# The FoX stage of a hybrid decoder block: engine order fixed by the source, weights as a stream of pieces, softmax in steps, heads as a pipeline, five gate units plain

## The chip, the cores and the metric

The kernel runs on one core of one Trainium2 chip. The time is the device time of one execution in microseconds (us), on that core. A core has five engines with a queue of their own each: TensorE (PE; matmuls, with PEld for its weight loads), VectorE (DVE), ScalarE (ACT), GpSimd (POOL) and SyncE (SP, which here only issues DMAs). In this kernel's programs every engine takes its instructions in the order of its own queue, and an instruction at the head that waits holds up all that stand behind it on that engine.

## The reference

One layer of a decoder trunk over 512 tokens behind 16 meta tokens, model width 1024. A normalised input `h` goes through one wide projection, whose columns are the inputs of two branches and of their gates:

```python
h = rms_norm(x, g_pre)
z = h @ w_in
(fq, fk, fv, ff, fz, mqk, mv, mi, mf, mo, mz, ga, gb) = jnp.split(z, SPLIT_POINTS, axis=-1)
oa = forgetting_attention(fq, fk, fv, log_fa)
ya = (oa * jax.nn.silu(fz)) @ w_a
hb = rms_norm(jax.nn.sigmoid(mo) * mlstm_scan(...), g_head)
yb = (hb * jax.nn.silu(mz)) @ w_b
merged = jax.nn.sigmoid(ga) * ya + jax.nn.sigmoid(gb) * yb
return x + rms_norm(merged @ w_o, g_post)
```

`forgetting_attention` (FoX) is causal softmax attention of 8 heads of 128, with a decay `cum[t] - cum[s]` added to the scores. The mLSTM branch has 4 heads with a matrix memory in chunks of 128.

## The kernel before

Everything is held transposed, channels on the 128 partitions and tokens along the free axis. Each fp32 operand is split into two parts of a shorter format, a high one (`_h`, a copy by ScalarE) and a low one (`_l`, a subtraction by VectorE), and a product is three matmuls, high by high, high by low and low by high (`mm3`, L148). A weight tile thus goes by DMA into a raw buffer (names in `_r`), through ScalarE and VectorE (`wsplit`, L141 and L143), and then to TensorE.

A block of 256 output columns over 512 tokens can be made in two ways. **Plain**: two banks of 512 columns, 2 x 8 x 3 = 48 matmuls of 512 columns. **Seven products** (`st_narrow`, L254, and `st_products`, L288): Strassen's scheme, 7 products of 12 matmuls of 256 columns, in the order X, Y, Z, W, Y, X, Z, on two banks. The weights are then split in four blocks, a to d; between them stand sums of raw blocks, two on GpSimd (L259, L260, before block b) and two on VectorE (L265, L266, before block d). Between the products ScalarE copies half-finished banks into a snapshot: a wide one behind the second product (512 columns, L313), a narrow one behind W (256 columns, L317) and one behind the second X (L321). A later product writes into the copied bank and has to wait for the copy. At the end VectorE combines the banks with the snapshots (L324, L325, L327).

The program runs the mLSTM branch head by head, with the blocks of `mz` (`mz_part`, L766) as seven-product units in it, then turns the last head's result (`turn_part`, L809) and comes to the FoX stage (L1018 on). This makes, with units of seven products for `fq`, `fz`, `ga` and `gb`, four pairs of heads: `fq_part` and `fk_part` (queries and keys of two heads), `fv_part` (values of four), then for each head the steps of the softmax:

- `prob_part` (L940): scores on TensorE (names `pl`); for each of four blocks of queries VectorE adds the decay `ab` and takes the least value (L959; the signs are turned), ScalarE takes the exponential (L964, with a running sum), VectorE the reciprocal (L965), and the product with it is written by GpSimd (a small part, L967) and VectorE (the rest, L969) into `pn`;
- `ptr_part` (L972): TensorE transposes `pn` into four banks `pt` and one `pmt`, ScalarE makes the high part `pth` (L986) and VectorE the low one `ptl` (L987);
- `fout_part` (L992): the product with the values (`pfo`), multiplied into `yb` by VectorE (L1005).

The gates' results wait in DRAM (`d_yb`, `d_sa`). After the stage come the product with `w_a` (names `pya`) and the output projection. Eight PSUM banks turn round among all of these; a bank is free when its last reader is done.

What sets the order: the source gives a program, and the framework's scheduler sorts the instructions of each engine by its own priorities, in front of the run. The order of the lines is a wish; buffers bind it (four raw buffers, four of `whi`, four of `wlo`, one of `whs` for block a).

## Time and profile before

| | us |
|---|---|
| median of 3 runs | 959.43 |
| lowest and highest | 958.69, 959.86 |
| the profiled execution's own time | 958.12 |
| its span | 956.3 |
| mLSTM part of the span, 110 to 516.8: length, PE busy | 406.80, 401.40 |
| tail, 861.1 to the end: length, PE busy | 95.20, 88.52 |

The profiled execution took 958.12 us, 1.8 us more than the span of its records. Times within the trace count from the span's start. The FoX stage begins with the first matmul of `fq0` at 516.8 and ends with the first one of `pya` at 861.1; its row, with the page's totals, is shown where it is used. Engines that overlap each have their own busy time, so these do not add up to the length of a stretch. In a view of waits a row gives who waited, for which instruction, the time in all, how often, and the longest.

### The profile page before, as it was taken

What the parts mean: (1) busy time and instruction counts of PE and PEld (TensorE: products, weight loads), DVE (VectorE), ACT (ScalarE), POOL (GpSimd) and SP (SyncE); (2) the same over time, 40 slices, a digit from 0 to 9 for tenths busy, and PEclk for the clock granted to TensorE, in tenths of its full rate; (3) what the DMA queues carried; (4) which work ended last, traced back from release to release, by engine and by line L of the source; (5) the groups of instructions that cost most, each with busy time, mean ns of one, the idle gap of its engine ahead of it and who ended that gap; (6) DMA issues with size and microseconds to landing.
All of it is one profiled execution on the core that took longest, in us unless ns stands there. A gap on an engine that the chain in (4) does not pass through costs nothing.

```text
span 956.3 us, 15752 instructions
## 1 busy us (share of the span) xinstructions
PE 915.8 (96%) x6296; PEld 844.5 (88%) x6296; DVE 649.0 (68%) x1080; ACT 473.9 (50%) x818; POOL 194.1 (20%) x222
## 2 busy tenths in 40 slices
PE   8999799999999999999999999989899999899997
PEld 6998799889998899988999988889798899798887
DVE  6988598447686276872768665677774676885633
ACT  5746456435565254662545424455653554773331
POOL 3055100120101211012112114223531233410000
PEclk9999999999999999999999999999999999999999
DMA  7323143203223222322223325224342233248402
GB/s 226 91 82 95 45 129 104 88 23 111 88 90 105 61 81 75 113 77 87 73 61 110 112 88 162 62 79 133 102 155 74 73 90 110 89 167 311 145 23 89
DMA packets 73539, 97.47 MB, mean 102 GB/s; under 512 B 5237, under 2 KB 56533, under 8 KB 73466
## 3 DMA queue, kind: packets, MB, share of 16 engines
q1 hardware_dynamic: 71400, 92.76, 31.7%
q0 software_dynamic: 576, 2.10, 0.6%
q10 hardware_dynamic: 1490, 1.61, 0.5%
q8 instruction: 49, 0.80, 0.3%
q14 instruction: 24, 0.20, 0.1%
HBM read 90.62 MB, written 5.83 MB: 101 GB/s over the span
## 4 chain that ended last, share of the span: by engine, by line
PE 73%; DVE 11%; issue 5%; POOL 5%; ACT 4%; DMA 1%; POOLq 0%; DVEq 0%; ACTq 0%
PE pyb L150 3%; PE pyb L151 3%; PE pyb L149 3%; PE pv L151 3%; PE pv L150 3%; PE pv L149 3%; PE po L149 3%; PE po L151 3%; PE po L150 3%; PE pqk L149 3%; PE pqk L151 3%; PE pqk L150 3%; PE pfk L149 2%; PE pfk L151 2%; PE pfk L150 2%
## 5 line engine op out<-in xcount | busy, mean ns | idle before, releaser
L967 POOL TENSOR_SCALAR pn<-lt,rsum 128x128 f32<-128x128 f32 x32 | 31.1, 972 | 108.6 <-DVE rsum L965 58.6
L150 PE MATMUL pyb<-bl,wb_h 128*128 128x512 f32 x128 | 49.9, 390 | 0.0
L151 PE MATMUL pyb<-bh,wb_l 128*128 128x512 f32 x128 | 49.8, 389 | 0.0
L149 PE MATMUL pyb<-bh,wb_h 128*128 128x512 f32 x128 | 49.8, 389 | 0.0
L150 PE MATMUL pv<-wv_l,hh 128*128 128x512 f32 (+1 forms) x128 | 46.6, 364 | 1.5 <-DVE wv_l L143 1.5
L151 PE MATMUL pv<-wv_h,hl 128*128 128x512 f32 (+1 forms) x128 | 46.4, 363 | 0.0
L149 PE MATMUL pv<-wv_h,hh 128*128 128x512 f32 (+1 forms) x128 | 46.4, 363 | 0.0
L694 DVE SCALAR_TENSOR_TENSOR y<-z,gc,y 128x512 f32<-128x512 f32 (+1 forms) x48 | 36.2, 759 | 2.0 <-ACT y L687 1.3
L149 PE MATMUL pqk<-hh,wq_h 128*128 128x258 f32 x128 | 36.4, 284 | 0.0
L149 PE MATMUL pfk<-hh,wfk_h 128*128 128x264 f32 x128 | 36.4, 284 | 0.0
L149 PE MATMUL pqk<-hh,wk_h 128*128 128x264 f32 x128 | 36.3, 284 | 0.0
L151 PE MATMUL pqk<-hh,wk_l 128*128 128x264 f32 x128 | 36.3, 284 | 0.0
L150 PE MATMUL pfk<-hl,wfk_h 128*128 128x264 f32 x128 | 36.3, 284 | 0.0
L151 PE MATMUL pfk<-hh,wfk_l 128*128 128x264 f32 x128 | 36.3, 283 | 0.0
L150 PE MATMUL pqk<-hl,wk_h 128*128 128x264 f32 x128 | 36.3, 283 | 0.0
L150 PE MATMUL pqk<-hl,wq_h 128*128 128x258 f32 x128 | 36.0, 282 | 0.0
L151 PE MATMUL pqk<-hh,wq_l 128*128 128x258 f32 x128 | 36.0, 282 | 0.0
L150 PEld LDWEIGHTS pv<-wv_l,hh 128*128 128x128 f32 x128 | 24.1, 189 | 5.6 <-DVE wv_l L143 1.7
L151 PEld LDWEIGHTS pyb<-bh,wb_l 128*128 128x128 f32 x128 | 24.0, 188 | 5.0
L149 PEld LDWEIGHTS pyb<-bh,wb_h 128*128 128x128 f32 x128 | 24.0, 188 | 4.9
L150 PEld LDWEIGHTS pyb<-bl,wb_h 128*128 128x128 f32 x128 | 24.0, 188 | 4.9
L149 PEld LDWEIGHTS pv<-wv_h,hh 128*128 128x128 f32 x128 | 24.2, 189 | 3.9
(1806 smaller groups left out, 3662.1 us busy)
## 6 DMA issues: line engine op xcount, KB each, us to landing
wv_r<-in_w_in_dram SPq DMA_DIRECT2D x16, 512.0 KB, 4.5
wo_r<-in_w_in_dram SPq DMA_DIRECT2D x16, 512.0 KB, 4.1
wz_r<-in_w_in_dram SPq DMA_DIRECT2D x16, 512.0 KB, 3.7
wb_r<-in_w_b_dram SPq DMA_DIRECT2D x16, 512.0 KB, 3.4
ab<-d_na SPq DMA_DIRECT2D x8, 672.0 KB, 3.8
wq_r<-in_w_in_dram SPq DMA_DIRECT2D x8, 512.0 KB, 3.6
wk_r<-in_w_in_dram SPq DMA_DIRECT2D x8, 512.0 KB, 3.7
wfq_r<-in_w_in_dram SPq DMA_DIRECT2D x8, 512.0 KB, 3.6
```

The costliest lines, as they stand in the source:

```text
L149: T.matmul(ps, ah, bh, start=start, stop=False, **kw)
L150: T.matmul(ps, ah, bl, start=False, stop=False, **kw)
L151: T.matmul(ps, al, bh, start=False, stop=stop, **kw)
L694: V.scalar_tensor_tensor(y[:, t0:L], z[:, m, t0 + j:L + j], gc[:, j * 16 + mi:j * 16 + mi + 1], y[:, t0:L], ALU.mult, ALU.add)
L967: G.tensor_scalar(pn[:, o:o + P].rearrange("p (g t) -> p g t", g=4), lt[:, 0:32].unsqueeze(1).to_broadcast([P, 4, 32]), rsum, None, ALU.mult)
```

## The change

Within the FoX stage, from `fq0` to the last product with `w_a`, each engine now keeps the order in which the source issues its instructions: `V`, `S`, `G` and `T` are wrapped, and each instruction that goes through them is pinned while `order["on"]` is set (in the trace they then all have the wrapper's line, L66).

The weights of the stage and of what follows it are one list of jobs. `loads()` starts the next DMA as soon as a raw buffer is spare, and `pieces()` issues the next piece of the list, a split with what belongs to it, if its buffers are free. `side(n)` stands between products: it takes up to n steps off the queue of the softmax and issues one piece. A unit of seven products calls it seven times, a plain one after each half of a row of products (four k each).

A head's softmax is cut into ten steps. Its scores, and the least value and exponential of the first two query blocks, are issued at once; the other steps go into the queue and are taken between the products that follow. The heads form a pipeline: in step s stand `fout_part` of head s-2, the scores of head s, the transposes of head s-1, and then the units of `INTERVALS[s]` (names with a star are units of seven products). `gb1`, `gb2`, `gb3`, `ga1` and `ga2` have no star: they are plain. The large part of the product with the reciprocal goes from VectorE to ScalarE, and the pair of banks of a unit is read from the second bank first. Snapshots of `fq` go into the buffer `sg` and not into `w`. Ahead of the stage one thing changes: every second block of `mz` puts its split a into `sg`, and four pieces of `fq0` are issued before `turn_part`. Of `w_a` the first block takes k 0 to 5 of both halves before k 6 and 7; the rest of the tail differs only in where its weights are loaded and split.

```diff
-    V, S, G, T = nc.vector, nc.scalar, nc.gpsimd, nc.tensor
+    order = {"on": False}
+
+    class Engine:
+
+        def __init__(self, engine):
+            self.engine = engine
+
+        def __getattr__(self, name):
+            issue = getattr(self.engine, name)
+            return lambda *a, **kw: tc.keep_in_program_order(issue(*a, **kw)) if order["on"] else issue(*a, **kw)
+
+    V, S, G, T = (Engine(e) for e in (nc.vector, nc.scalar, nc.gpsimd, nc.tensor))
...
     def mz_part(h, u):
         g = sb([P, 2, SEQ], F32, ("qk1h", "qk1l")[u], f"gz{h}{u}")
-        ps = st_unit(C_MZ + h * MV + u * 256, f"z{h}{u}", g)
+        ps = banks(f"pz{h}{u}", 2)
+        snap = g.rearrange("p a (b n) -> p (a b) n", b=2)
+        into = None
+        if u:
+            t = sb([P, 2, 4, P], F32R, "sg", f"wz{h}{u}a", gp)
+            into = t[:, 0], t[:, 1]
+        st_products(st_narrow(C_MZ + h * MV + u * 256, f"wz{h}{u}", into), [(ps[0], ps[1], snap, None)])
...
+    class Job:
+        def __init__(self, name, src, k0, nk, c0, nc_, seven=False):
+            self.name, self.src, self.k0, self.nc, self.c0, self.seven = name, src, k0, nc_, c0, seven
+            self.hk = 1024 // nc_
+            self.n = nk // self.hk
+            self.raws, self.done, self.parts = [], 0, {}
+            self.pieces = 4 if seven else self.n
...
+        def piece(self):
+
+            i = self.done
+            pool = "whs" if self.seven and i == 0 else "whi"
+            if not spare[pool] or len(self.raws) < (2 if self.seven else i + 1):
+                return False
+            spare[pool] -= 1
+            if not self.seven:
+                self.parts[i] = split(self.raws[i], f"{self.name}{i}")
+                spare["raw"] += 1
...
+                if i == 0:
+                    self.parts["a11"] = split(r0[:, :, a], f"{self.name}a", ("whs", "wls"), mw, 1)
+                    G.tensor_tensor(r0[:, :, a], r0[:, :, a], r0[:, :, b], ALU.add)
+                    G.tensor_tensor(r0[:, :, b], r0[:, :, b], r1[:, :, b], ALU.add)
+                elif i == 1:
+                    self.parts["s3"], self.parts["s1"] = both(r0, "b")
+                elif i == 2:
+                    self.parts["a12"], self.parts["a22"] = both(r1, "c")
+                    V.tensor_tensor(r1[:, :, b], r0[:, :, a], r1[:, :, b], ALU.add)
+                    V.tensor_tensor(r1[:, :, a], r1[:, :, a], r1[:, :, b], ALU.add)
+                    spare["raw"] += 1
+                else:
+                    self.parts["s4"], self.parts["s2"] = both(r1, "d")
+                    spare["raw"] += 1
+            self.done += 1
+            return True
...
+    INTERVALS = (("gb1",), ("fq1*", "fk1", "fv0", "fz0*"), ("gb2",), ("fq2*", "fk2", "fz1*"), ("gb3",),
+                 ("fq3*", "fk3", "fv2", "fz2*", "fz3*"), ("ga1",), ("ga2",), ("ga3*",))
+    add("gb0*", *(n for i in INTERVALS for n in i))
...
+    def loads():
+        while loading[0] < len(jobs) and spare["raw"]:
+            j = jobs[loading[0]]
+            if len(j.raws) < j.n:
+                j.load()
+                spare["raw"] -= 1
+            else:
+                loading[0] += 1
+
+    def pieces():
+        loads()
+        while splitting[0] < len(jobs) and jobs[splitting[0]].done == jobs[splitting[0]].pieces:
+            splitting[0] += 1
+        ok = splitting[0] < len(jobs) and jobs[splitting[0]].piece()
+        loads()
+        return ok
+
+
+    queue = []
+
+    def side(n=1):
+        if order["on"]:
+            for _ in range(n):
+                if queue:
+                    queue.pop(0)()
+            pieces()
...
+    def plain(job, ps):
+
+        w = job.w()
+        for m in range(2):
+            for k in range(KC):
+                mm3(ps[m], w[0](k, m * P, m * P + P), w[1](k, m * P, m * P + P),
+                    hh[:, k, NM:L], hl[:, k, NM:L], k == 0, k == KC - 1)
+                if k % 4 == 3:
+                    side(3)
+        free(n=2)
+        return ps
...
+        prod("X", "a11", "b11", 0)
+        free("whs")
+        side(2)
+        prod("Y", "s3", "t3", 1)
+        S.activation(snap[:, 0:2], halves(yx), AF.Copy)
+        side(2)
+        prod("Z", "s1", "t1", 1)
+        free()
+        side(2)
+        prod("W", "a12", "b21", 2)
+        S.activation(snap[:, 3], wz[:, 256:512], AF.Copy)
+        side(2)
+        prod("Y", "a22", "t4", 2)
+        free()
+        side()
+        prod("X", "s2", "t2", 3)
+        S.activation(snap[:, 2], yx[:, 256:512], AF.Copy)
+        side()
+        prod("Z", "s4", "b22", 3)
+        free()
+        V.tensor_tensor(yx[:, 256:512], snap[:, 0], yx[:, 256:512], ALU.subtract)
+        V.tensor_tensor(halves(yx), halves(yx), snap[:, 2:4], ALU.subtract)
+        V.tensor_tensor(halves(wz), halves(wz), snap[:, 1:3], ALU.add)
+        side()
+        return ps
...
     def fq_part(p):
-        ps = st_unit(C_FQ + p * 256, f"fq{p}", sb([P, 2, SEQ], F32, "w", f"fqs{p}"))
+        ps = unit(by_name[f"fq{p}"], room(f"fqs{p}"))
...
+        def normal(c):
+            kn, o = ends(c)[-1][1], OFFP[c]
+            S.activation(pn[:, o + P:o + P + kn - NM], lts[c][:, NM:kn], AF.Identity, scale=rsums[c])
...
-            V.tensor_scalar(pn[:, o + P:o + P + kn - NM], lt[:, NM:kn], rsum, None, ALU.mult)
+                            lts[c][:, 0:32].unsqueeze(1).to_broadcast([P, 4, 32]), rsums[c], None, ALU.mult)
...
+        for c in (0, 1):
+            scores(c)
+            least(c)
+            power(c)
+        for c in (2, 3):
+            scores(c)
+        more += [lambda: inverse(0), lambda: normal(0), lambda: (least(2), inverse(1)),
+                 lambda: (power(2), normal(1)), lambda: (least(3), after()), lambda: (power(3), inverse(2)),
+                 lambda: normal(2), lambda: inverse(3), lambda: normal(3)]
+        if h + 1 < FH:
+            more.append(lambda: ab_mask(abs_[h + 1]))
...
+    for _ in range(4):
+        pieces()
+    bt = turn_part(*pend)
+    order["on"] = True
     q = fq_part(0)
+    abs_[0] = ab_load(0)
...
+    ab_mask(abs_[0])
...
     gb_part(0)
...
+    pns, pts, vs = {}, {}, {}
+    gs = []
+    for s in range(FH + 2):
+        flush()
+        if s >= 2:
+            fout_part(s - 2, pts[s - 2], vs[(s - 2) // 4])
+        if s < FH:
+            pns[s] = prob_part(s, q, k, queue)
+        if 1 <= s <= FH:
+            pts[s - 1] = ptr_part(s - 1, pns[s - 1])
+        if s == FH:
+            for p in range(2):
+                gs.append(gsplit(p, (sb([P, 2, SEQ], F32R, f"qk{p}h", f"gh{p}"),
+                                     sb([P, 2, SEQ], F32R, f"qk{p}l", f"gl{p}"))))
+            gs.append(gsplit(2, pair("w", "g2")))
+        for n in INTERVALS[s] if s < len(INTERVALS) else ():
+            kind, u = n[0:2], int(n[2])
+            if kind == "fq":
...
-    sa3 = gate_part(C_GA, 3, "ga")
...
-        w2 = wchunk(wa, 0, KC, u * 256, 256, f"wa{u}")
+        w2 = by_name[f"wa{u}"].w()
...
+        for ks in (range(6), range(6, 8)) if u == 0 else (range(8),):
+            for m in range(2):
...
+    order["on"] = False
```

Three places show how the order moves. In the rows, `wfq1d_h` is the high part of block d of unit `fq1`'s weights, `fqs1` its snapshot, `lt1c`, `mn1c` and `rsum1c` the scores, least value and sum of query block c of head 1, and a number behind the last underscore names the buffer.

**First place: unit `fq1`, ScalarE.** Before:

```order
L927 ACTIVATE sgb1_6586<-pgb1_1_6588 128x512
L249 ACTIVATE wfz1a_h_7033<-wfz10_r0_7029 128x512
L313 ACTIVATE fqs1_6722<-pfq1_1_6724 128x512
L141 ACTIVATE wfk1_h1_6853<-wfk1_r1_6847 128x1024
L317 ACTIVATE fqs1_6722<-pfq1_0_6723 128x256
L249 ACTIVATE wfz1b_h_7039<-wfz10_r0_7029 128x1024
L321 ACTIVATE fqs1_6722<-pfq1_1_6724 128x256
L249 ACTIVATE wfz1c_h_7043<-wfz11_r0_7031 128x1024
```

After:

```order
L66 ACTIVATE pn1_6268<-lt10_6273,rsum10_6276 128x128
L66 ACTIVATE wfq1d_h_6349<-wfq1_r1_6039 128x1024
L66 ACTIVATE fqs1_6331<-pfq1_1_6333 128x512
L66 ACTIVATE lt12_6368,rsum12_6372<-lt12_6368,mn12_6369 128x400
L66 ACTIVATE pn1_6268<-lt11_6282,rsum11_6285 128x256
L66 ACTIVATE wfk10_h_6376<-wfk1_r0_6058 128x1024
L66 ACTIVATE lt13_6394,rsum13_6400<-lt13_6394,mn13_6395 128x528
L66 ACTIVATE wfk11_h_6403<-wfk1_r1_6076 128x1024
L66 ACTIVATE fqs1_6331<-pfq1_0_6332 128x256
```

Before, the narrow snapshot (`fqs1`, 256 columns, from bank 0) had one split between it and the wide one. Now two exponentials (`lt12`, `lt13`), a product with the reciprocal and two splits stand between them.

VectorE at the same place, before:

```order
L251 TENSOR_TENSOR wfq1d_l_6747<-wfq11_r0_6727,wfq1d_h_6745 128x1024
L143 TENSOR_TENSOR wfk1_l0_6851<-wfk1_r0_6845,wfk1_h0_6849 128x1024
L1005 TENSOR_TENSOR yb_75<-pfo1_6707,yb_75 128x512
L251 TENSOR_TENSOR wfz1a_l_7035<-wfz10_r0_7029,wfz1a_h_7033 128x512
L143 TENSOR_TENSOR wfk1_l1_6855<-wfk1_r1_6847,wfk1_h1_6853 128x1024
L251 TENSOR_TENSOR wfz1b_l_7041<-wfz10_r0_7029,wfz1b_h_7039 128x1024
L324 TENSOR_TENSOR pfq1_1_6724<-fqs1_6722,pfq1_1_6724 128x256
```

And after:

```order
L66 RECIPROCAL rsum10_6276<-rsum10_6276 128x1
L66 TENSOR_TENSOR wfq1d_l_6351<-wfq1_r1_6039,wfq1d_h_6349 128x1024
L66 ISA lt12_6368,mn12_6369<-pl120_6287,ab1_6226 128x400
L66 ISA mn12_6369 128x1
L66 RECIPROCAL rsum11_6285<-rsum11_6285 128x1
L66 TENSOR_TENSOR wfk10_l_6378<-wfk1_r0_6058,wfk10_h_6376 128x1024
L66 ISA lt13_6394,mn13_6395<-pl130_6291,ab1_6226 128x264
L66 ISA mn13_6395 128x1
L66 ISA lt13_6394,mn13_6395<-pl131_6295,ab1_6226,mn13_6395 128x264
```

Before, no step of a softmax stood among the low parts of this unit. Now the third and fourth query blocks' least values (the rows `lt12` and `lt13`) stand there, the fourth behind the low part of `wfk10`.

**Second place: the end of unit `fz0` and the step behind it, VectorE.** `pfz0_0` and `pfz0_1` are the unit's banks, `yb_75` takes its result. Before:

```order
L265 TENSOR_TENSOR wgb11_r0_6591<-wgb10_r0_6589,wgb11_r0_6591 128x4x128
L266 TENSOR_TENSOR wgb11_r0_6591<-wgb11_r0_6591 128x4x128
L324 TENSOR_TENSOR pfz0_1_6420<-yb_75,pfz0_1_6420 128x256
L325 TENSOR_TENSOR pfz0_1_6420<-pfz0_1_6420,yb_75 128x512
L327 TENSOR_TENSOR pfz0_0_6419<-pfz0_0_6419,yb_75 128x512
L251 TENSOR_TENSOR wgb1d_l_6611<-wgb11_r0_6591,wgb1d_h_6609 128x1024
L921 TENSOR_TENSOR yb_75<-pfz0_0_6419,yb_75 128x512
L921 TENSOR_TENSOR yb_75<-pfz0_1_6420,yb_75 128x512
L1005 TENSOR_TENSOR yb_75<-pfo0_6539,yb_75 128x512
L987 TENSOR_TENSOR ptl1_6555<-pt10_6558,pth1_6554 128x128
```

After:

```order
L66 TENSOR_TENSOR wfq2a_l_6831<-wfq2_r0_6697,wfq2a_h_6829 128x512
L66 TENSOR_TENSOR wfq2b_l_6849<-wfq2_r0_6697,wfq2b_h_6847 128x1024
L66 TENSOR_TENSOR pfz0_1_6766<-yb_75,pfz0_1_6766 128x256
L66 TENSOR_TENSOR pfz0_1_6766<-pfz0_1_6766,yb_75 128x512
L66 TENSOR_TENSOR pfz0_0_6765<-pfz0_0_6765,yb_75 128x512
L66 TENSOR_TENSOR wfq2c_l_6881<-wfq2_r1_6731,wfq2c_h_6879 128x1024
L66 TENSOR_TENSOR wfq2_r1_6731<-wfq2_r0_6697,wfq2_r1_6731 128x4x128
L66 TENSOR_TENSOR wfq2_r1_6731<-wfq2_r1_6731 128x4x128
L66 TENSOR_TENSOR yb_75<-pfz0_1_6766,yb_75 128x512
L66 TENSOR_TENSOR yb_75<-pfz0_0_6765,yb_75 128x512
L66 TENSOR_TENSOR yb_75<-pfo0_6891,yb_75 128x512
L66 ISA lt20_6911,mn20_6912<-pl200_6907,ab2_6398 128x144
```

The combinations of the banks now stand behind two low parts of the next `fq`, and one low part and two sums stand between them and the products that free the banks. The product of `pfo` and the least value of head 2 come next, ahead of the low parts of the transposes.

**Third place: unit `fq0`, ScalarE.** `bh` is the high part of the last mLSTM head's turned result. Before:

```order
L249 ACTIVATE wga0a_h_5743<-wga00_r0_5739 128x512
L313 ACTIVATE fqs0_5491<-pfq0_1_5493 128x512
L141 ACTIVATE wfk0_h1_5622<-wfk0_r1_5616 128x1024
L820 ACTIVATE bh3_5439<-yt30_5446 128x4x128
L820 ACTIVATE bh3_5439<-yt31_5456 128x4x128
L317 ACTIVATE fqs0_5491<-pfq0_0_5492 128x256
L249 ACTIVATE wga0b_h_5749<-wga00_r0_5739 128x1024
L820 ACTIVATE bh3_5439<-yt32_5466 128x4x128
```

After:

```order
L66 ACTIVATE gz31_5318<-pz31_1_5320 128x512
L66 ACTIVATE bh3_5477<-yt30_5484 128x4x128
L66 ACTIVATE bh3_5477<-yt31_5494 128x4x128
L66 ACTIVATE bh3_5477<-yt32_5504 128x4x128
L66 ACTIVATE bh3_5477<-yt33_5514 128x4x128
L66 ACTIVATE wfk00_h_5534<-wfk0_r0_5449 128x1024
L66 ACTIVATE fqs0_5519<-pfq0_1_5521 128x512
L66 ACTIVATE wfk01_h_5565<-wfk0_r1_5451 128x1024
L66 ACTIVATE fqs0_5519<-pfq0_0_5520 128x256
```

The wide snapshot of `fq0` (`fqs0`, 512 columns) stood ahead of all four `bh`; it now stands behind them and a split of `wfk`.

269 lines of the change are left out of this document (180 added, 89 removed).

## The prediction

> **What bounds the kernel now.** I read the page's busy shares and clock first, then the window of the changed stage, then what TensorE's weight loads waited for there and in the stage ahead of it.
>
> ```profile
> span 956.3 us, 15752 instructions
> PE 915.8 (96%) x6296; PEld 844.5 (88%) x6296; DVE 649.0 (68%) x1080; ACT 473.9 (50%) x818; POOL 194.1 (20%) x222
> PEclk9999999999999999999999999999999999999999
> ...
> 516.80:861.10 344.30, 325.42 (x2386) 306.70 (x2385) 241.85 (x423) 181.26 (x314) 103.23 (x98) 1.00 0.35 109
> ```
>
> TensorE is busy for 96% of the span at a granted clock that no slice shows below nine tenths; in the FoX window (columns: length, then busy us of PE, PEld, DVE, ACT, POOL) the clock is 1.00. So there are two ways to gain: fewer matmuls, or fewer gaps. In the FoX window PE is idle for 344.30 - 325.42 = 18.9 us, while VectorE (241.85) and ScalarE (181.26) are far from full: its gaps are latencies of chains, not a full engine. The waits of the weight loads, FoX window first, the window 110 to 516.8 behind it:
>
> ```profile
> PEld pfz L149 <- ACT yb L317: 7.5, 4, 2.4
> PEld pga L149 <- ACT sga L317: 4.0, 2, 2.2
> PEld pgb L149 <- issue: 3.9, 2, 2.0
> PEld pl L149 <- DVE ptl L987: 2.3, 2, 1.1
> PEld pgb L149 <- ACT sgb L317: 1.8, 1, 1.8
> PEld pl L149 <- DVE mn L959: 1.7, 2, 0.8
> ...
> PEld pz L149 <- ACT gz L317: 4.9, 7, 1.0
> PEld pht L816 <- PE pz L151: 1.6, 2, 0.8
> PEld pz L149 <- ACT gz L313: 0.8, 1, 0.8
> ```
>
> The first six rows add up to 21.2 us, a little more than the 18.9, since a gap also costs the filling of the array. The largest kind is a seven-product unit that waits for its own snapshot (L317), which stands on ScalarE behind a weight split that waited for GpSimd's sums. The reader should see that this wait is made by the order on ScalarE, so another order can take it away, or make another.
>
> **The change, part by part.** It takes no matmul away from the stage; it adds some, and it swaps one set of in-order queues for another.
>
> *Five plain units.*
>
> ```profile
> L149 PE MATMUL pfz<-hh,wfz0a_h x4: 280/280/282, 613.1 to 614.2; 128*128 128x256 f32 x4
> L149 PE MATMUL pfz<-t3h,wfz0b_h x4: 276/276/282, 614.5 to 615.6; 128*128 128x256 f32 x4
> ...
> 554.70 0.39 PE L151 MATMUL pyb<-bh,wb_l 128*128 128x512 f32 x1
> 555.38 0.39 PE L151 MATMUL pyb<-bh,wb_l 128*128 128x512 f32 x1
> ```
>
> The first product of a unit begins at 613.1 and the next at 614.5, so one product is 1.4 us and seven are 9.8. A 512-column matmul is started every (555.38 - 554.70)/3 = 0.227 us, so 48 of them are 10.9. Each plain unit is 1.1 us longer: **+5.5** for gb1, gb2, gb3, ga1 and ga2. This lies on TensorE itself and nothing can hide it. In exchange these five have no snapshot to wait for and fewer VectorE operations.
>
> *The old gaps go:* **-21.2**, if nothing follows them. In the new order the snapshot of W (before, L317) stands ahead of the split that waits for GpSimd in every unit.
>
> *The mLSTM stage:* a block of `mz_part` gets its own buffer for the first split, and the scheduler moves these splits ahead; the waits for gz are 4.9 + 0.8 = 5.7. The order on ScalarE still has the snapshot of two of the seven units behind a wait, so I take **-4.5** (bounds 0 and -7.3, all three rows).
>
> *New waits in FoX.* Rows for the durations, of ScalarE, then VectorE, then GpSimd (busy, mean ns, idle before):
>
> ```profile
> L964 ACT ACTIVATE lt<-lt,mn 128x144 f32<-128x144 f32 (+3 forms) x32 | 18.2, 570 | 10.6 <-DVE mn L959 9.9 <-DVE rsum L965 0.4
> L141 ACT ACTIVATE wfk_h<-wfk_r 128x1024 fp32r<-128x1024 f32 x8 | 8.5, 1067 | 0.1
> L964 ACT ACT_TABLE_LOAD x6 | 7.7, 1283 | 0.1
> L986 ACT ACTIVATE pth<-pt 128x128 fp32r<-128x128 f32 (+3 forms) x32 | 11.9, 449 | 0.3 <-ACT pth L986 0.3
> L927 ACT ACTIVATE sgb<-pgb 128x512 f32<-128x512 f32 x8 | 4.3, 589 | 2.3 <-DVE pgb L327 2.3
> L317 ACT ACTIVATE fqs<-pfq 128x256 f32<-128x256 f32 x4 | 1.6, 392 | 1.0 <-PE pfq L151 1.0
> ...
> L143 DVE TENSOR_TENSOR wfk_l<-wfk_r,wfk_h 128x1024 fp32r<-128x1024 f32 x8 | 9.7, 1218 | 0.0
> L959 DVE CUSTOM_DVE_ANT_0 lt<-pl,ab 128x144 f32<-128x144 f32 (+3 forms) x32 | 13.4, 437 | 6.6 <-POOL pn L967 5.3 <-PE pfz L150 1.0
> L959 DVE CUSTOM_DVE_ANT_0 lt<-pl,ab,mn 128x264 f32<-128x264 f32 x8 | 3.9, 486 | 0.2
> L969 DVE TENSOR_SCALAR pn<-lt,rsum 128x128 f32<-128x128 f32 (+3 forms) x32 | 16.3, 509 | 0.7
> L921 DVE TENSOR_TENSOR yb<-pfz,yb 128x512 f32<-128x512 f32 x8 | 5.1, 686 | 1.8 <-ACT yb L920 1.8
> ...
> L259 POOL TENSOR_TENSOR wfq_r<-wfq_r 128x512 f32<-128x512 f32 x3 | 3.9, 1291 | 15.0 <-DVE wfq1a_l L251 7.5 <-DVE wfq3a_l L251 7.5
> ```
>
> *fq1, fq2, fq3.* Set 0 where the four transposes of the head before are done. ScalarE first copies pth and ptm, then makes pn (c=0) at about 2.1, the split wfq_d 1.07, the wide snapshot 0.6: 4.0. VectorE's least(2) follows wfq_d's low part and is done at 5.2; power(2) 0.7, normal(1) 0.4 and the split of wfk's first half 1.07 end at 7.3; VectorE takes the low part (1.2) and only then least(3), 0.43 + 0.49 and its two read-outs: 9.6; power(3) 0.8, the second half's split 1.07, and then the snapshot of W, 0.4: 11.8. TensorE has done six products by 6 x 1.4 = 8.4 and needs that snapshot for the seventh. So **3.4** each, 10.2 for three. (Before, this unit's snapshot came right behind one split.) Bounds 0, if the low parts run ahead, and 5.
>
> *fz0 and fz1, then the transposes.* Set 0 at the unit's last product. wfq_a's split is issued at about -3.8; its low part, two GpSimd sums of 1.29 and wfq_b's split end at +1.2, then the last snapshot at 1.5, three combinations of the banks to 3.2, another low part (1.2) and two sums (0.69 each) to 5.8, and only then the two multiplications of L921 that free the banks: 7.1. TensorE, behind pfo (2.1) and the scores (2.0), wants these banks at 4.1: 3.0 lost. Behind it stand the multiplication of pfo, least(0), least(1), power(0), power(1), four pth and the ptl that free the next unit's banks, some 1.8 late: **4.8** each, 9.6 for two; bounds 1 and 6.2.
>
> *fq0.* Its wide snapshot now stands behind four bh conversions, which wait for VectorE's yt and bl, and behind wfk's split.
>
> ```profile
> 521.21 0.58 ACT L313 ACTIVATE fqs<-pfq 128x512 f32<-128x512 f32 x1
> 523.40 1.16 ACT L820 ACTIVATE bh<-yt 128x512 fp32r<-128x512 f32 x2 [0.66 <-DVE yt L819]
> 530.93 0.62 ACT L820 ACTIVATE bh<-yt 128x512 fp32r<-128x512 f32 x1
> ```
>
> Before, the snapshot was at 521.21 and the last bh at 530.9. With nothing else between them VectorE's chain of yt, bl, yt lets the last bh end at about 525.4; the split and the snapshot then end at 527.0. The unit starts at 516.8 and its fifth product is due four products later, at 522.4: 4.6 late. The split of wfq0 is earlier in the new order, so VectorE reaches this chain some 0.9 sooner: **3.7** (bounds 0 and 4.6).
>
> *gb1, then the transposes of head 0 and fq1.* Both sigmoids (2 x 0.59), a table load 1.28, two exponentials, four pth and the last ptl, some 6.6 in all, against scores and transposes of 3.6: **3.0** (0 to 4). The remaining seams (fz2 to fz3, ga1, ga2, ga3) I price at **2.5** together (0 to 5).
>
> The normalisation that goes from VectorE (509 ns, 32 times) to ScalarE adds 16 us to an engine that has 163 free, and is in the chains above.
>
> **A rule weighed.** ScalarE's list has 16 table loads in FoX instead of 12; three of the chains above pass one. The row has six at 1283 ns each, with 0.1 us of idle time before all six. The Trainium skill (ScalarE: Activation LUTs, What ACT_TABLE_LOAD costs) gives the same 1283 ns for the load, and puts a drain of about 1380 ns to every switch. By that rule the four more switches would cost up to 5.5 us beyond their loads, an estimate from that page, and the sum would be some 5 us higher; the row shows no such drain as idle time, and my sum goes by the row.
>
> **The sum.** -21.2 - 4.5 + 5.5 + 10.2 + 9.6 + 3.7 + 3.0 + 2.5 = +8.8. Against the profiled execution of 958.1 (span 956.3 and 1.8 around it) that is 966.9. The median of the runs, 959.4, lies 1.3 above the profiled one, so I say 968.
>
> **The rivals.**
> - *The queues give enough cover.* ScalarE and VectorE are idle for 163 and 102 us of the stage; five units less to combine leave more. Should the steps run a product earlier than in my walk, the fq and gb1 waits go, and half of fq0 and fz stays: 3.7/2 + 9.6/2 = 6.7; with the other terms, -21.2 - 4.5 + 5.5 + 6.7 = -13.5, or 946. For it: the old gaps came from an order that no source line wrote. Against it: least(3) and L921 are behind low parts in the queue itself, and these wait for ScalarE.
> - *Half of it.* Only the fq waits go: 968 - 10.2 = 958, no change.
> - *VectorE and GpSimd slow each other.* GpSimd's sum took 1291 ns for wfq, and the row of wga has 1805; the pass of VectorE that lies beside it can stretch too. If each of the seven fq and fz units left in the intervals loses 1.5 so, 968 + 7 x 1.5 = 978. Against it: the new order puts the low part ahead of the sum that waits for it.
> - *The switches of tables are not covered.* Four more loads of 1.28 us, each on a chain that TensorE waits for, are 5.1: 968 + 5.1 = 973. Against it: I have three of them in the walk, and the others stand where ScalarE has time to spare.
> - *The change does nothing.* The order on each engine is different from the first row of the stage on, so I give this no chance of its own.
>
> **How the numbers follow.** My forecast (slower, 962 to 975 its own range) 0.46; cover 0.26, around 946; half 0.18, 953 to 962; contention 0.07, about 978; uncovered table switches 0.03, 973. About 0.2% (1.9 us) is what a measurement of this kernel can tell from no change. Faster: 0.26 and half of the third case, 0.09, so 0.35; within 0.2%: the third case's other half, 0.09; slower: the rest, 0.56. The range runs from 945 to 977: it leaves out the lower part of the cover case, about 0.12, and the upper part of contention, 0.05.
>
> **What would show it.** Right: waits of TensorE for the narrow snapshot of fq1, fq2, fq3 of about 3 us each, for a bank of pfz behind fz0 and fz1, and one of the wide snapshot in fq0; no wait for a snapshot in ga0 and fz0 to fz2; plain units of 10.9. Wrong: PE idle under 10 us from the start of fq0 to the first pya (the cover case), or fq units of 9.8 without a gap (the half case), or GpSimd's sums well above 1.3 us (contention).

## The result and the profile after

| | before | after |
|---|---|---|
| median of the runs, us | 959.06 (4 runs, 957.69 to 959.86) | 985.70 (4 runs, 985.11 to 986.32) |
| ratio after to before | | 1.0279 (95% interval 1.0262 to 1.0297) |
| profiled execution: span, mean granted clock of TensorE | 956.3, 0.999 | 983.3, 0.973 |

The change makes the kernel slower by 26.6 us, where the prediction had 9 more and a range that ended at 977. The sign and the places of the new waits were right; a whole cost was missing. The page of the kernel after:

```profile
span 983.3 us, 15369 instructions
PE 936.0 (95%) x6116; PEld 856.8 (87%) x6116; DVE 615.3 (63%) x1013; ACT 481.6 (49%) x829; POOL 168.1 (17%) x212
PEclk9999799999999999999999999998998899999999
```

TensorE is busy 20.2 us longer (936.0 against 915.8) with 180 fewer matmuls, and the clock row has digits under 9 in the fifth slice and in the second half. Both are signs that the matmuls themselves were slower. Where the time went is read by windows of both kernels, cut at the same four places of the program: the start of the first mz unit, the start of `fq0`, the start of `pya`. After (columns: length, then busy us of each engine, clock, DMA):

```profile
0.00:116.70 116.70, 106.59 (x676) 94.01 (x677) 91.19 (x166) 64.17 (x112) 35.42 (x49) 0.94 0.37 110
116.70:514.30 397.60, 396.84 (x2759) 369.86 (x2758) 276.31 (x430) 203.74 (x350) 54.33 (x68) 1.00 0.29 86
514.30:888.10 373.80, 344.00 (x2207) 316.00 (x2206) 202.69 (x356) 188.42 (x325) 76.16 (x92) 0.95 0.33 103
888.10:983.30 95.20, 88.54 (x481) 76.96 (x480) 45.08 (x64) 25.33 (x44) 2.22 (x4) 0.98 0.38 128
```

And before, the two stretches that were not shown yet:

```profile
0.00:112.00 112.00, 102.48 (x676) 90.11 (x677) 89.66 (x164) 62.61 (x110) 36.28 (x51) 1.00 0.39 115
112.00:516.80 404.80, 399.40 (x2759) 370.67 (x2758) 272.02 (x431) 204.53 (x351) 52.41 (x70) 1.00 0.28 83
```

The difference of 27.0 us between the spans is +4.7 ahead of the first mz unit, -7.2 in the mLSTM part behind it, +29.5 in FoX, and nothing in the tail. FoX divides further. TensorE's idle time grew from 18.9 to 373.8 - 344.0 = 29.8, which is +10.9. Its busy time grew by 18.6, of which the five plain units are 5.5; the other **13.1 us are matmuls that ran slower**. TensorE's waits in FoX after the change:

```profile
PE pfq L66 <- ACT fqs L66: 14.8, 4, 4.6
PE pt L66 <- DVE yb L66: 7.8, 4, 3.6
PE pmt L66 <- DVE mn L66: 3.6, 1, 3.6
PE pfz L66 <- ACT yb L66: 2.3, 1, 2.3
PE pga L66 <- ACT sga L66: 0.8, 1, 0.8
PE pmt L66 <- DVE yb L66: 0.3, 2, 0.2
PE pga L66 <- DVE ptl L66: 0.2, 1, 0.2
```

These are the predicted places: the snapshots of `fq0` to `fq3`, the banks behind `fz0` and `fz1`, the first transposes. In sum they are 29.8 us, where the prediction added up 29.0. What came with them is seen where `fq1` waits, in TensorE's timeline (start, duration, what, idle time before it):

```profile
613.69 0.28 PE L66 MATMUL pfq<-t2l,wfq1d_h 128*128 128x256 f32 x1
613.80 0.28 PE L66 MATMUL pfq<-t2h,wfq1d_l 128*128 128x256 f32 x1
617.20 0.58 PE L66 MATMUL pfq<-hh,wfq1d_h 128*128 128x256 f32 x1 [3.12 <-ACT fqs L66]
617.58 0.41 PE L66 MATMUL pfq<-hl,wfq1d_h 128*128 128x256 f32 x1
617.79 0.41 PE L66 MATMUL pfq<-hh,wfq1d_l 128*128 128x256 f32 x1
```

A matmul of the same form takes 0.28 us ahead of the wait and 0.41 behind it, and they start 0.21 us apart instead of 0.11. The windows behind four of the waits give the granted clock (last but two):

```profile
103.30:115.00 11.70, 10.63 (x38) 8.93 (x39) 6.71 (x15) 4.87 (x10) 0.10 (x1) 0.50 0.16 46
524.80:528.10 3.30, 3.30 (x16) 3.30 (x17) 2.52 (x3) 1.66 (x3) 0.43 (x1) 0.52 0.37 130
617.20:620.20 3.00, 3.00 (x14) 3.00 (x15) 1.21 (x3) 2.35 (x5) 0.95 (x2) 0.51 0.81 259
774.40:780.60 6.20, 6.20 (x29) 6.20 (x30) 4.37 (x7) 4.26 (x7) 3.30 (x5) 0.50 0.71 224
```

The clock is half, for 3 to 6 us behind these waits in FoX and for 11.7 us behind the wait that began at 98.8 us. Eight waits in this kernel, of 3.1 to 4.6 us, have such a stretch behind them, seven of them in FoX; a ninth, of 2.3 us in `fz3`, has none. In all the clock of the FoX stage is halved for 34.1 us, in 3.6 of which TensorE is idle. Half of the other 30.5 is 15.2, a little more than the 13.1 that are left over in the sum above; where the difference comes from stays open.

### The profile page after: what moved, and what is told of

It is laid out like the page before. It is cut to its first block, busy times and chain, and to the rows that moved or that the text cites. A ratio compares the mean times of both kernels' runs of the same rounds, so it can differ in the third digit from the quotient of the medians.

```text
span 983.3 us, 15369 instructions
## 1 busy us (share of the span) xinstructions
PE 936.0 (95%) x6116; PEld 856.8 (87%) x6116; DVE 615.3 (63%) x1013; ACT 481.6 (49%) x829; POOL 168.1 (17%) x212
## 4 chain that ended last, share of the span: by engine, by line
PE 77%; DVE 9%; ACT 7%; issue 3%; POOL 2%; DMA 1%; POOLq 0%; DVEq 0%; ACTq 0%; SPq 0%
PE pyb L66 9%; PE pv L66 8%; PE pqk L66 8%; PE po L66 6%; PE pz L66 6%; PE pfk L66 5%; PE pgb L66 5%; PE pfv L66 4%; PE pya L66 4%; PE pout L66 4%; PE pga L66 4%; PE pfz L66 3%; PE pnb L66 2%; PE pna L66 2%; PE ps L66 2%
## 5 line engine op out<-in xcount | busy, mean ns | idle before, releaser
L66 PE MATMUL pv<-wv_l,hh 128*128 128x512 f32 (+1 forms) x128 | 46.6, 364 | 1.5 <-DVE wv_l L66 1.5
L66 PE MATMUL pv<-wv_h,hl 128*128 128x512 f32 (+1 forms) x128 | 46.4, 363 | 0.0
L66 PE MATMUL pv<-wv_h,hh 128*128 128x512 f32 (+1 forms) x128 | 46.4, 362 | 0.0
L66 POOL TENSOR_SCALAR pn<-lt,rsum 128x128 f32<-128x128 f32 x32 | 20.3, 634 | 106.5 <-DVE rsum L66 106.5
L66 PE MATMUL pfk<-hh,wfk_h 128*128 128x264 f32 x128 | 37.5, 293 | 0.0
L66 PE MATMUL pyb<-bh,wb_l 128*128 128x512 f32 x96 | 37.4, 389 | 0.0
L66 PE MATMUL pyb<-bl,wb_h 128*128 128x512 f32 x96 | 37.4, 389 | 0.0
L66 PE MATMUL pyb<-bh,wb_h 128*128 128x512 f32 x96 | 37.4, 389 | 0.0
L66 DVE SCALAR_TENSOR_TENSOR y<-z,gc,y 128x512 f32<-128x512 f32 (+1 forms) x48 | 36.0, 754 | 2.2 <-ACT y L66 1.5
L66 PE MATMUL pfk<-hl,wfk_h 128*128 128x264 f32 x128 | 37.1, 290 | 0.0
L66 PE MATMUL pfk<-hh,wfk_l 128*128 128x264 f32 x128 | 37.1, 290 | 0.0
L66 PE MATMUL pqk<-hh,wq_h 128*128 128x258 f32 x128 | 36.4, 284 | 0.0
L66 PE MATMUL pqk<-hh,wk_h 128*128 128x264 f32 x128 | 36.3, 283 | 0.0
L66 PE MATMUL pqk<-hh,wk_l 128*128 128x264 f32 x128 | 36.3, 283 | 0.0
L66 PE MATMUL pqk<-hl,wk_h 128*128 128x264 f32 x128 | 36.2, 283 | 0.0
L66 PE MATMUL pqk<-hh,wq_l 128*128 128x258 f32 x128 | 36.0, 282 | 0.0
L66 PE MATMUL pqk<-hl,wq_h 128*128 128x258 f32 x128 | 36.0, 282 | 0.0
L66 PE MATMUL pout<-wwo_h,m 128*128 128x256 f32 (+1 forms) x144 | 33.5, 318 | 0.0
L66 ACT ACTIVATE lt<-lt,mn 128x144 f32<-128x144 f32 (+3 forms) x32 | 18.3, 573 | 30.6 <-DVE rsum L66 20.8
L66 ACT ACTIVATE gz<-pz 128x512 f32<-128x512 f32 (+1 forms) x40 | 20.0, 507 | 18.7 <-PE pz L66 12.7
L66 PEld LDWEIGHTS pv<-wv_l,hh 128*128 128x128 f32 x128 | 24.1, 189 | 5.6 <-DVE wv_l L66 1.7
```

Of the source, the lines that this page charges most:

```text
L66: return lambda *a, **kw: tc.keep_in_program_order(issue(*a, **kw)) if order["on"] else issue(*a, **kw)
```

## The experiments

Each kernel is the one after the change with the edit shown, unless it says otherwise; times are medians, the ratio is to the kernel before on the same chip. The table has the profiled execution of each: when the first mz unit begins, and for the FoX stage its length, TensorE's busy and idle time, and how much of the stage has a granted clock of one half, all in us.

| kernel | first mz unit at | FoX | busy | idle | at half clock |
|---|---|---|---|---|---|
| before | 112.0 | 344.3 | 325.4 | 18.9 | 0 |
| after | 116.7 | 373.8 | 344.0 | 29.8 | 34.1 |
| `e1_fill` | 115.5 | 381.8 | 349.6 | 32.2 | 30.7 |
| `e7_fill` | 115.7 | 368.6 | 347.7 | 20.9 | 23.9 |
| `e2_steps` | 115.9 | 358.1 | 338.6 | 19.5 | 27.3 |
| `e4_fq0` | 115.9 | 372.5 | 346.2 | 26.3 | 34.1 |
| `e5_fz` | 116.2 | 371.7 | 342.1 | 29.6 | 23.9 |
| `e8_gb0` | 117.0 | 373.1 | 343.3 | 29.8 | 30.7 |
| `e3_mz` | 113.4 | 373.1 | 344.4 | 28.7 | 34.1 |
| `e11_stars` | 115.5 | 411.8 | 353.7 | 58.1 | 61.4 |
| `e12_normal` | 114.8 | 366.5 | 340.7 | 25.8 | 27.3 |
| `e9_all` | 112.1 | 351.9 | 337.7 | 14.2 | 10.2 |
| `e10_best` | 111.9 | 346.9 | 334.8 | 12.1 | 3.4 |
| `e13_tail` | 112.2 | 368.0 | 340.7 | 27.3 | 23.9 |
| `e14_bestv` | 112.0 | 338.9 | 332.2 | 6.7 | 0 |

Half clock comes and goes in steps of 3.41 us (the last section shows why), and one step more or less is some 1.7 us of work. The first mz unit begins between 114.8 and 117.0 us in the eight of these kernels whose source up to there is that of `after`. So some 2 us of a difference can come from where the clock's steps fell, and not from the edit.

### Filling the waits

`e1_fill` and `e7_fill` leave the waits of `fq0` to `fq3` and only give TensorE something to do in them: matmuls with zero weights that add nothing to a finished half of a bank.

```diff
+    def fill(bank):
+        for _ in range(18):
+            T.matmul(bank[:, 0:256], zero[:, 0:P], zero, start=False, stop=False, skip_group_check=True)
...
+        if job.name == "wfq0":
+            fill(wz)
         prod("Y", "a22", "t4", 2)
```

> 18 matmuls with zero weights stand ahead of the product that waits in fq0, fq1, fq2 and fq3; they add zero to a finished half of a bank, so the result stays. Theory (a wait of some 3.3 us or more halves TensorE's granted clock, which costs about 1.5 us behind each): the four waits still end when they ended, but the matmuls behind them take 0.28 us and not 0.41, the granted clock stays at 1.00 there, and the time falls by 4 x 1.5 = 6, to about 980. Rival (the matmuls behind the waits are slow because the DMAs of the next weights, at over 270 GB/s there, or the other engines disturb them): they still take 0.41, and the time stays at 986.

993.1 us (ratio 1.0368, 1.0337 to 1.0398), slower by 7. The edit missed its aim: the snapshot reads the bank that the zero matmuls write, so these waited for it as well and came on top. TensorE's idle time in FoX is 2.4 us longer and not shorter. In `e7_fill` the call stands ahead of the snapshot in the program, where the bank has no reader yet:

```diff
         prod("X", "s2", "t2", 3)
+        if job.name in ("wfq1", "wfq2", "wfq3"):
+            fill(yx)
         S.activation(snap[:, 2], yx[:, 256:512], AF.Copy)
```

In `fq0` it stands in the same way behind W, ahead of the narrow snapshot.

> As in e1_fill, but the 18 zero matmuls stand one activation earlier, so nothing holds them up: they run in the first 2 us of the waits in fq0, fq1, fq2 and fq3, which otherwise stay. Theory (TensorE's clock halves behind a stretch of some 3.3 us or more without a matmul): the waited products start when they did, the stretches without a matmul are 1.4 to 2.8 us, the matmuls behind them take 0.28 us and not 0.41, and the time falls by 4 x 1.5 = 6, to about 980. Rival (DMAs or other engines slow the matmuls behind the waits): still 0.41 there, 986.

978.4 us (1.0195, 1.0179 to 1.0210): 7.3 less for work that nobody needs. In the profiled executions FoX is 5.2 shorter, and 1.0 more lies ahead of the first mz unit, where the edit does nothing. The half clock behind the waits of `fq1`, `fq2` and `fq3`, 13.7 us in the kernel after, is gone; in `fq0` a wait of 2.6 us is left, and 3.4 us at half clock with it. In `fq2` the zero matmuls end 1.60 us ahead of the product that waits, and the matmuls behind it are fast from the second one on:

```profile
703.75 0.93 PE L66 MATMUL pfq<-zero 128*128 128x256 bf16 x7
706.28 0.38 PE L66 MATMUL pfq<-hh,wfq2d_h 128*128 128x256 f32 x1 [1.60 <-ACT fqs L66]
706.50 0.28 PE L66 MATMUL pfq<-hl,wfq2d_h 128*128 128x256 f32 x1
```

The windows behind the waits of `fq2` and `fq3` show the full clock while the DMAs move as much as ever:

```profile
706.20:709.00 2.80, 2.72 (x22) 2.73 (x23) 1.78 (x3) 1.78 (x4) 0.94 (x1) 1.00 0.80 268
770.90:773.50 2.60, 2.51 (x20) 2.51 (x21) 1.10 (x2) 1.95 (x4) 0.60 (x1) 1.00 0.90 307
```

So the rival (DMAs or other engines slow the matmuls) falls: with 268 and 307 GB/s beside them the matmuls run at full rate where TensorE has not stood still for long. The halved clock is the price of the idle stretch.

### Taking single waits away

`e2_steps`: the softmax steps are popped only behind the snapshot of W; three calls `side(2)` in `seven` become:

```diff
-        side(2)
+        side(0)
```

> In a unit of seven products the softmax steps are taken only behind the narrow snapshot of W, and pieces as before. Theory (the snapshot of fq1, fq2, fq3 is late because exponentials and least values stand ahead of it on ScalarE and VectorE): the three waits of 3.3 to 3.7 us go, and with them 3 x 1.5 us at half clock: 10.7 + 4.5 = 15 less, about 970. Rival (the softmax is late anyway): the wait turns up behind fk, at the transposes or at the scores of the next head, and the time is above 980.

969.0 us (1.0106, 1.0089 to 1.0123), 16.7 less. Of the first row above only the wait of `fq0` is left, and nothing has come in its place:

```profile
PE pt L66 <- DVE yb L66: 7.8, 4, 3.6
PE pfq L66 <- ACT fqs L66: 4.6, 1, 4.6
```

Three waits were 14.8 - 4.6 = 10.2 us, and TensorE's idle time in FoX fell by 10.3. Its busy time fell by 5.4 with the same matmuls; of this the half clock, 27.3 us in place of 34.1, makes some 3.4. This is the chain of the prediction's `fq` step, shown by taking it apart.

`e4_fq0`: the last mLSTM head's result is turned behind `fq0`.

```diff
-    bt = turn_part(*pend)
     order["on"] = True
     q = fq_part(0)
+    bt = turn_part(*pend)
```

> The last mLSTM head's result is turned behind fq0, and not ahead of it, so the four bh conversions no longer stand ahead of the wide snapshot of fq0. Theory: the wait of 4.7 us in fq0 and 1.5 us at half clock go: 6 less, about 980. Rival (the snapshot waits for the end of mz, or the wait turns up at the transposes or in the products with w_b): less than 2 us, 984 or more.

978.5 us (1.0206, 1.0185 to 1.0227), 7.2 less. `fq0` took 10.8 us and not 16.3; a wait of 1.0 for `fql` in `fk0` is new. The half clock behind `fq0` is gone, but FoX has 34.1 us of it as before: behind the other waits some stretches are a step longer and some a step shorter, and `fz3` now has one. So the time came out near the forecast, but not by both of its terms.

`e5_fz`: in `fz0` and `fz1` the calls of `side` behind W are left out, so the next unit's pieces come in the plain unit.

```diff
+        late = job.name not in ("wfz0", "wfz1")
+        if late:
+            side(2)
...
-        side()
+        if late:
+            side()
```

> In fz0 and fz1 no piece of the next fq is issued behind the product W; they come in the plain unit that follows. Theory (the banks of fz come free late because a low part and two sums stand ahead of the multiplications on VectorE): the waits of 3.8 us in the scores behind fz0 and fz1 go, with them the 1.2 us in the transposes and 1.5 us at half clock, some 6 each, 12 in all: 974. Rival (the sigmoids behind their table load decide, or the plain unit then waits for the pieces): 982 or more.

980.8 us (1.0214, 1.0197 to 1.0231), 4.9 less, not 12. The 3.6 us behind `fz0` and `fz1` fell to under 1, but the pieces then stood in VectorE's queue beside a softmax, and `fq2` and `fq3` began late instead:

```profile
695.39 0.39 PE L66 MATMUL pfq<-hh,wfq2a_h 128*128 128x256 f32 x1 [1.56 <-DVE ptl L66]
```

The theory holds for the place and not for the sum: the idle time in FoX is 29.6 us against 29.8, so what these waits gave was lost again in others one step later. The gain is in the half clock, 23.9 us against 34.1.

`e8_gb0`: `gb0` stands behind the scores of head 0.

```diff
-    INTERVALS = (("gb1",), ("fq1*", "fk1", "fv0", "fz0*"), ("gb2",), ("fq2*", "fk2", "fz1*"), ("gb3",),
+    INTERVALS = (("gb0*", "gb1"), ("fq1*", "fk1", "fv0", "fz0*"), ("gb2",), ("fq2*", "fk2", "fz1*"), ("gb3",),
...
-    add("gb0*", *(n for i in INTERVALS for n in i))
+    add(*(n for i in INTERVALS for n in i))
...
-    gb_part(0)
```

> gb0 goes behind the scores of head 0 instead of ahead of them, so that head 0 has the length of two units and not of one for its softmax. Theory (the first transposes wait 3.8 us because the softmax of head 0 and then the decay row of head 1, whose one buffer is free only when head 0's last least value is done, take longer than gb1): that wait and 1.5 us at half clock go, 980. Rival (the sigmoids of gb1 and their two table loads are what the transposes wait for): the wait shrinks by less than 1 us, 985.

984.1 us (1.0252, 1.0236 to 1.0267), 1.6 less, which the intervals don't tell from no change. The wait of 3.6 at the transposes is gone. In its place `fq1` waits 1.3 at its start for a low part of the transposes, and a wait of 1.5 for a snapshot in `gb0`, which now has softmax steps in it, is new; with the snapshots of `fq0` and `fq1`, which came 0.6 us later together, the idle time in FoX is 29.8 as before. In the kernel after, VectorE shows what the least values of head 1 waited for, the decay row behind its DMA:

```profile
601.91 0.31 DVE L66 CUSTOM_DVE_ANT_0 lt<-pl,ab 128x144 f32<-128x144 f32 x1 [3.39 <-POOL ab L66]
```

So at this seam the prediction had a wait of about the right length from a wrong cause: it counted sigmoids and table loads, not the one buffer of `ab`. What the four more table loads of FoX cost by themselves was not isolated.

`e3_mz`: `if u:` becomes `if u and h:`, so head 0 has no early split.

> The second mz block of head 0 puts its split a into its old buffer again; heads 1 to 3 keep the new one. Theory (the early split of wz01 made the one wait at 98.5 us longer, from 3.2 to 4.5, and so put it over the limit of the clock): the first mz unit begins at about 112 us instead of 116.7, the clock from 100 to 125 us is 1.00, and the time falls by some 4.5, to 981. Rival (the wait is longer for another reason, by the order that the scheduler took): no change, 986.

981.8 us (1.0242, 1.0220 to 1.0265), 3.9 less, near the number but not by the mechanism. The first mz unit begins at 113.4 and not at 116.7, yet the wait at 98.8 us is still 4.3 (4.5 with the early split, 3.2 before), and the clock behind it is still halved, for 6.8 us in place of 13.7:

```profile
PE ps L66 <- ACT yb L66: 4.3, 1, 4.3
...
103.30:108.70 5.40, 5.40 (x19) 4.82 (x20) 3.23 (x8) 2.95 (x8) 0.00 (x0) 0.50 0.33 97
```

In the later kernels with the same edit it was 2.9 to 3.5. So the early split isn't shown to be the cause of the long wait; what the scheduler's order in this stretch adds, and what was only the place of the clock's steps, stays open.

### Parts of the change by themselves

`e11_stars`: the five plain units are units of seven products again (a star on each name).

> The kernel after the change with gb1, gb2, gb3, ga1 and ga2 as units of seven products again. If the plain form only costs its 1.1 us each, the time falls by 5.5, to 980. Rival (these five follow a head's scores, as fq does, so their snapshots stand behind the same softmax steps): waits of 3 us or more turn up in them, with 1.5 us at half clock each, 5 x (3.4 + 1.5 - 1.1) = 19 more, about 1005.

1022.0 us (1.0656, 1.0627 to 1.0684): 36 more, beyond even the rival. The snapshots in `gb1` to `gb3` now wait, and the transposes more than before:

```profile
PE pt L66 <- DVE yb L66: 14.1, 9, 4.7
PE pgb L66 <- ACT sgb L66: 13.0, 5, 5.7
```

The plain form is no loss in this order: its 5.5 us keep five more units from standing behind the softmax steps.

`e12_normal`: the large part of the product with the reciprocal goes back to VectorE.

```diff
-            S.activation(pn[:, o + P:o + P + kn - NM], lts[c][:, NM:kn], AF.Identity, scale=rsums[c])
+            V.tensor_scalar(pn[:, o + P:o + P + kn - NM], lts[c][:, NM:kn], rsums[c], None, ALU.mult)
```

> The kernel after the change with the large part of the product with the reciprocal on VectorE, as before the change. In fq the chain to the narrow snapshot passes one such product (0.4 us) on ScalarE; on VectorE it stands ahead of the next low part. Theory (it is one small term of the chain on either engine): within 3 us of 985.7. Rival (ScalarE's 16 us more are what makes the waits): the waits in fq fall by over 1 us each and the time to 975 or less.

977.3 us (1.0197, 1.0180 to 1.0214), 8.4 less: outside the theory's 3 us, and 2 short of the rival. The waits in `fq1` to `fq3` went from 3.1, 3.6 and 3.6 down to 2.3, 2.2 and 2.2. In the profiled executions FoX is 7.3 shorter, 4.0 of it idle time and 3.3 busy time, with 27.3 us at half clock in place of 34.1; the first mz unit begins 1.9 earlier, to which the edit adds nothing. The shorter waits don't leave the clock alone as such: behind `fq1` it stayed full, behind `fq2` and `fq3` it was halved for 3.4 us each (the last section shows the like in `fz3`). So one product per block cost some 7 us: 4.0 as longer waits, the rest as half clock, and how much of that rest is the edit's and how much the place of the clock's steps isn't shown.

### Together

`e9_all` has the edits of `e2_steps`, `e3_mz`, `e4_fq0`, `e5_fz` and `e8_gb0`.

> The edits of e2_steps, e3_mz, e4_fq0, e5_fz and e8_gb0 together. If each takes away its own wait and the half clock behind it, 985.7 less 16.7, 3.9, 7.2, 12 and 5 is 941, which beats the kernel before by 18. Rival (the waits hand on to the next shortage, since ScalarE and VectorE are given work no sooner in sum): 955 or more.

956.0 us (0.9956, 0.9940 to 0.9973). That is 30 less than the kernel after and a little less than the kernel before, but 15 over the sum of the expected parts and so the rival's number: `e5_fz` and `e8_gb0` had given 7.1 and 3.4 less than expected, and `fz3` still waits 2.3 us and then runs at half clock.

`e10_best` puts `fv2` between `fz2` and `fz3`:

```diff
-                 ("fq3*", "fk3", "fv2", "fz2*", "fz3*"), ("ga1",), ("ga2",), ("ga3*",))
+                 ("fq3*", "fk3", "fz2*", "fv2", "fz3*"), ("ga1",), ("ga2",), ("ga3*",))
```

> e9_all with fv2 between fz2 and fz3, which stood back to back. Theory (the wide snapshot of fz3 waits 2.5 us behind the sigmoids of fz2 and their table load, and the clock then halves): that wait and its 1.7 us at half clock go, 956 - 4.1 = 952. Rival (the sigmoids or the pieces of fz3 now hold up fv2): no gain, 956.

952.1 us (0.9936, 0.9918 to 0.9954), as expected.

`e13_tail` gives `ga1` and `ga2` their stars in that kernel.

> e10_best with ga1 and ga2 as units of seven products. If only their length counts: 2 x 1.1 less than e10_best. Rival (as in e11_stars, the snapshots stand behind softmax steps; with the steps behind W this is ga1 alone, since ga2 has no head's steps beside it): 1 to 5 us more than e10_best.

972.3 us (1.0138, 1.0118 to 1.0157), 20 more, far beyond both. With the steps behind W a unit of seven products takes only five of a head's ten steps; the rest is issued at the next head's start, right ahead of the transposes that need it:

```profile
861.27 0.90 PE L66 MATMUL pt<-ident,pn 128*128 128x128 f32 x3 [6.40 <-ACT pn L66]
```

`e14_bestv` is `e10_best` with the product on VectorE.

> e10_best with the large part of the product with the reciprocal on VectorE. The waits left in the fq units of e10_best are at their start, for the low part of the transposes, and no longer at the narrow snapshot. If ScalarE's share matters only through that snapshot (theory), nothing is left to gain: 952 within 2. Rival (ScalarE's 16 us are late anywhere in a step): 948 or less.

943.4 us in 5 runs (0.9840, 0.9827 to 0.9854), 8.7 less than `e10_best`: the rival, and the fastest kernel of the study, 15.4 below the one before on the same chip. Its span and its FoX window:

```profile
span 941.3 us, 15354 instructions
...
507.70:846.60 338.90, 332.16 (x2223) 304.39 (x2222) 212.91 (x390) 176.45 (x296) 83.22 (x93) 1.00 0.36 114
```

In FoX TensorE is idle for 6.7 us, against 12.1 in `e10_best` (346.90 long, 334.81 busy) and 18.9 before the change. So ScalarE's share is late in more places than the one snapshot. FoX is 8.0 shorter, 5.4 of it idle time.

## Why the prediction was wrong

**What bounds the kernel:** right. TensorE carried the time, and other engines were costly where it waited for them.

**The sum of the waits:** right. Predicted were 10.2 + 9.6 + 3.7 + 3.0 + 2.5 = 29.0 us in FoX, measured 29.8. By place (time idle): `fq1` to `fq3` 3.1, 3.6 and 3.6 for 3.4 each; behind `fz0` and `fz1` 3.6 at the first transpose and some 0.4 in those that follow, for 4.8 each; `fq0` 4.6 for 3.7; the first transposes 3.6 for 3.0, from another cause; the other seams 2.3 + 0.8 + 0.2 for 2.5. In `fq1` ScalarE's timeline goes step by step as the prediction walked it; from the end of the wide snapshot to the end of the narrow one it takes 7.9 us, for 7.8 in the walk:

```profile
608.65 0.60 ACT L66 ACTIVATE fqs<-pfq 128x512 f32<-128x512 f32 x1
610.77 0.63 ACT L66 ACTIVATE lt<-lt,mn 128x400 f32<-128x400 f32 x1 [1.52 <-DVE rsum L66]
...
615.10 0.73 ACT L66 ACTIVATE lt<-lt,mn 128x528 f32<-128x528 f32 x1 [2.26 <-DVE rsum L66]
...
616.78 0.36 ACT L66 ACTIVATE fqs<-pfq 128x256 f32<-128x256 f32 x1
```

**The step that failed: each wait was priced at its own length.** In the kernel before, the waits in FoX were 2.4 us at most, and the clock stood at full; the prediction took that clock for granted while it summed up waits of 3 us and more. Behind those the clock was halved for 3.4 or 6.8 us each, and the matmuls took up to twice as long there. `e7_fill` shows it by leaving the waits and taking the idle stretches out of them: 13.7 us less at half clock behind three of them, and 7.3 us less in all. In FoX it is 13.1 us. The stretch at 103 to 115 us, whose wait no step of the prediction looked at, adds most of 4.7 (TensorE busy 106.59 against 102.48 there). The Trainium skill (TensorE: Matmul & The Clock Gate, What's actually happening) states it: an idle window of about 3.4 us gates the clock to half, a busy one of that length opens it again, and the windows run freely. The half (0.50) and the steps of 3.41 us in these traces agree with it; but a window need not be idle throughout: 2.3 of 3.41 us were enough, as the last section shows, and there the measurement decides. By that rule the six waits that the prediction put at 3.4 us or more (in `fq0` to `fq3`, and behind `fz0` and `fz1`) would have been seen as a cost of about 1.7 us each, half of such a window, which is an estimate from that page; it was the rule to weigh against this change, and not the one on table loads.

**Sizes that were off.** The old gaps could give 18.9, the idle time of the stage, and not the 21.2 of the weight loads' waits. The mLSTM part gained 7.2 and not 4.5; 4.6 of it is idle time, and why its matmuls were busy for 2.6 less stays open. The five plain units add 5.5 by the spacing of the matmuls; that the change adds matmuls holds for their time, not for their number, which falls by 180. The normalisation's move to ScalarE, which had 163 us free, was counted only as 0.4 us in the `fq` chains; going back is worth 8.4 in `e12_normal` and 8.7 in `e14_bestv`, of which 7.3 and 8.0 lie in FoX: free time in a stage says nothing about an instruction that stands ahead of a snapshot in an in-order queue. The rival of contention had the nearest time, 978, and was not what happened: GpSimd's sums of weights in FoX took 1.28 to 1.29 us each after the change, where its sign was sums well above 1.3.

The sum again, with measured terms: idle time in FoX +10.9, plain units +5.5, half clock in FoX +13.1, early stretch +4.7, mLSTM part -7.2: 27.0. From the prediction's 8.8 to this it is 2.3 for the old gaps, 0.8 for the new ones, -2.7 for the mLSTM part, and 13.1 and 4.7 for what had no term.

## What to carry to other kernels

Price a wait of TensorE by its length and by what the clock does behind it: in this kernel a stretch of over 3 us without a matmul mostly cost 3.4 or 6.8 us at half clock on top. By the same rows two waits of under 2 us should be cheaper than one of 4, which no run here compares directly. Where a long wait can't be avoided, some matmuls without effect in it can pay for themselves, if they don't write a bank whose reader stands ahead of them. When an order is fixed by hand, look along each in-order queue at what stands ahead of the copies that TensorE waits for; steps without a hurry belong behind them, in units that have no such copy. And a piece of work moved to the engine with more free time is not free if it comes to stand in a chain.
